# Other accumulators in a Strassen-like down projection, with the halves of the contraction exchanged

## The chip, the cores and the metric

One core of a Trainium2 chip runs the whole program. The metric is the device time of one execution in microseconds, as the median of several runs. Five engines matter: TensorE (PE, with its weight loads as PEld), VectorE (DVE), ScalarE (ACT), GpSimd (POOL) and SyncE (SP), which issues most of the DMAs. Each works through its own queue in a fixed order and waits for the others by semaphores.

## The reference, cut to what matters

An encoder of two layers runs on 512 + 256 tokens with 1024 channels. Each layer has two feed-forward blocks around a token mixer, so there are four in all:

```python
def swiglu_ffn(x, w1, w2):
    gate, up = jnp.split(x @ w1, 2, axis=-1)
    return (jax.nn.silu(gate) * up) @ w2

x = x + 0.5 * swiglu_ffn(rmsnorm(x, norm_g[li, 0]), ffn_w1[li, 0], ffn_w2[li, 0])
...
x = x + 0.5 * swiglu_ffn(rmsnorm(x, norm_g[li, 2]), ffn_w1[li, 1], ffn_w2[li, 1])
```

Here `w1` is 1024 x 5632 and `w2` is 2816 x 1024, in fp32. The change is in the second product, hidden @ w2, and in how its operands are laid out.

## The kernel before

**Precision.** Each fp32 operand is split into a high and a low part: ACT casts the high part (L199 for weights, L266 for activations) and DVE subtracts it from the value for the low part (L200, L267). A product of two operands is three matmuls: high by high, high by low, low by high.

**Seven products for eight.** The 768 tokens are halved (H = 384, that is HB = 3 blocks of 128), and so are the contraction and the outputs. A product of 2 x 2 blocks is made of seven block products, p1 to p7, as in Strassen's method in Winograd's form. Some operands are plain blocks, others are sums of blocks. On the activation side `FACTOR` (L45) names them: p1, p2 and p3 take the plain blocks b00, b10 and b11; p5, p6, p7 and p4 take t1, t2, t3 and t4, which `mix` (L348) makes with four subtractions, each followed by a split. In `b{j}{half}`, j is the half of the contraction and `half` the half of the tokens. Block b01 is used only inside the sums.

On the weight side `quad_steps` (L172) gets four raw tiles, a11, a12, a21 and a22, and three sums are made by accumulating DMAs that POOL issues (`into`, L140): two tiles s3 += a11, and a21 += a22. Seven steps then split one weight each. Two of them alter a tile for later steps: `p1` splits a11 and then adds a21 to it (L206); `p2` splits a12 and then adds a11 to it (L210). So p3, which splits a12, has the right value only after p1 and p2; p4 splits a22, p5 the sum in a21, p6 the altered a11, p7 the two s3 tiles.

**Staging.** Weights are staged in the order in which they were planned. `ahead` (L244), called by `done` whenever a product has used its weight, stages the next one as long as no more than WBUFS = 8 tiles are held. A weight of the up projection takes one tile, one of the down projection two. Raw tiles are four (RAWBUFS), and a down quad needs all four; they come free as the steps that read them are done, and then SP loads the next quad (L151).

**Up projection.** `up_pair` (L431) makes gate and up for one block of 128 hidden channels: seven products of 12 matmuls (L421) into four PSUM banks, with copies, sums, the Silu (L442, L454) and the multiplications (L449, L455) between. It yields two tiles, the first token half before its last product, the second after it. Four such tiles (two channel blocks, two token halves) go through `put` and `mix` as one part `kp` of the operands of the down projection.

**Down projection.** Every 512 hidden channels make a group (five in each feed-forward, 20 in all), and `down_quad` (L458) multiplies them by their rows of w2: seven products in the order `DOWN`, each of 3 token blocks x 2 parts x 3 = 18 matmuls (L479). After each product and block, `add_x` (L501, DVE) adds the bank, times 0.5 or -0.5, into a quarter of x. Three products continue in the bank of an earlier one, so that the sum of both is added to another quarter: p2 continues p1, p4 continues p5, and p3 continues p7. A continuing product must wait until `add_x` has read the bank. x is held in a transformed state over the five groups of a feed-forward: in the first group DVE alters two quarters (L464, L465), in the last it takes this back (L494, L495).

The order in which the engines get their instructions is fixed when the program is built. It follows the code, but an instruction that the builder reckons ready may be set ahead of one that waits.

Of the kernel before, what the change touches and what calls it, by code (L numbers as in the profile page):

```python
# [35 lines left out]
HB = H // P  # L36
# [4 lines left out]
SLOTS = 21  # L41
RING = 1024
UP = ("p1", "p7", "p2", "p5", "p4", "p6", "p3")
DOWN = ("p1", "p2", "p5", "p4", "p7", "p6", "p3")
FACTOR = {"p1": "b00", "p2": "b10", "p3": "b11", "p4": "t4", "p5": "t1", "p6": "t2", "p7": "t3"}  # L45


class Trunk:
# [291 lines left out]
    def put(self, name, kp, src):  # L340
        t = self.ops[(name, kp)] = self.big([P, 2, 2, H], F32R)
        self.split(src, t[:, :, 0, :], t[:, :, 1, :])
# [5 lines left out]
    def mix(self, b11, b12, b21, b22, put):  # L348
        sub = self.nc.vector.tensor_sub
        sub(b22, b12, b22)  # L350
        sub(b12, b11, b12)
        put("t1", b12)
        sub(b11, b11, b22)
        sub(b21, b21, b11)  # L354
        put("t4", b21)
        put("t3", b22)
        put("t2", b11)

    def sums(self):
        for kp in range(2):  # L360
# [17 lines left out]
    def plan_ffn(self, tag, w1, w2):  # L378
        def up(i):
            gate, up = (w1[:, c * P : (c + 1) * P] for c in (i, NF + i))  # L380
            if i < PLAIN:
                self.plan((tag, i, 0), gate, (NC, P))
                self.plan((tag, i, 1), up, (NC, P))
            else:
                self.plan_quad((tag, i), (gate, up), (NC, P), UP)

        for g in range(GROUPS):
            for i in range(4 * g, 4 * g + 4):
                up(i)
            rows = w2[4 * g * P : (4 * g + 4) * P, :].rearrange("(a k p) c -> k p a c", p=P, k=2)  # L390
            srcs = [rows[k][:, :, c * 512 : (c + 1) * 512] for c in range(2) for k in range(2)]
            self.plan_quad((tag, "down", g), srcs, (2, 512), DOWN)
        for i in range(NF - 2, NF):
            up(i)
        for c in range(2):
            self.plan((tag, "last", c), w2[(NF - 2) * P :, c * 512 : (c + 1) * 512], (2, 512))
# [61 lines left out]
    def down_quad(self, tag, g, hid):  # L458
        nc = self.nc
        cols = lambda b, c: self.x[b][:, c * 512 : (c + 1) * 512]  # L460
        if g == 0:
            for i in range(HB):
                x12, x21, x22 = cols(HB + i, 0), cols(i, 1), cols(HB + i, 1)
                nc.vector.tensor_add(x12, x12, x22)  # L464
                nc.vector.tensor_sub(x21, x21, x22)  # L465
        banks = {}
        for name in DOWN:
            wh, wl = self.take((tag, "down", g, name))
            chain = {"p2": "p1", "p4": "p5", "p3": "p7"}.get(name, name)
            for i in range(HB):  # L470
                if name == chain:
                    banks[(chain, i)] = self.ps()
                ps = banks[(chain, i)]
                sl = slice(i * P, (i + 1) * P)
                for kp in range(2):
                    h = hid[FACTOR[name]]
                    a, w = (h[:, kp, 0, sl], h[:, kp, 1, sl]), (wh[:, kp, :], wl[:, kp, :])
                    for q, (x, y) in enumerate(((0, 0), (0, 1), (1, 0))):
                        nc.tensor.matmul(  # L479
                            ps,  # L480
                            a[x],
                            w[y],
                            start=name == chain and kp == 0 and q == 0,
                            stop=kp == 1 and q == 2,
                            skip_group_check=True,
                        )
                x22 = cols(HB + i, 1)
                dst = {"p2": cols(i, 0), "p4": cols(i, 1), "p3": cols(HB + i, 0)}.get(name, x22)
                self.add_x(dst, ps, -0.5 if name in ("p1", "p5") else 0.5)
            self.done((tag, "down", g, name))  # L490
        if g == GROUPS - 1:
            for i in range(HB):
                x12, x21, x22 = cols(HB + i, 0), cols(i, 1), cols(HB + i, 1)
                nc.vector.tensor_sub(x12, x12, x22)  # L494
                nc.vector.tensor_add(x21, x21, x22)  # L495

    def add_x(self, x, ps, c):
# [5 lines left out]
    def ffn(self, tag, next_row):  # L503
        for g in range(GROUPS):
            hid = {}

            def put(name, src, kp):
                if name not in hid:
                    hid[name] = self.big([P, 2, 2, H], F32R)
                self.split(src, hid[name][:, kp, 0, :], hid[name][:, kp, 1, :])  # L510

            def gather(ts, kp):
                self.mix(ts[0], ts[1], ts[2], ts[3], lambda name, src: put(name, src, kp))

            if g == 0:
                ts = {}
                for half in range(2):
                    for j in range(PLAIN):
                        t = ts[2 * j + half] = self.up_plain(tag, j, half)
                        name = f"b{j}{half}"  # L520
                        if name != "b01":
                            put(name, t, 0)
                gather(ts, 0)
                self.run_later(len(self.deferred))
            for kp in range(2):
                if g == 0 and kp == 0:
                    continue
                ts = []
                for j in range(2):
                    for half, t in enumerate(self.up_pair(tag, 4 * g + 2 * kp + j)):  # L530
                        ts.append(t)
                        name = f"b{j}{half}"
                        if name != "b01":
                            put(name, t, kp)
                gather(ts, kp)
            self.down_quad(tag, g, hid)
        hids = []
        for j in range(NF - 2, NF):
            hid = self.big([P, 2, T], F32R)
            for half, t in enumerate(self.up_pair(tag, j)):  # L540
                self.split(t, *(hid[:, i, half * H : (half + 1) * H] for i in range(2)))
            hids.append(hid)
        if next_row is None:
            self.load_final()
        banks = {}

        def add(b, k, hid):
            sl = slice(b * P, (b + 1) * P)
            for c in range(2):
                wh, wl = self.take((tag, "last", c))  # L550
                if k == 0:
                    banks[(b, c)] = self.ps()
                w = wh[:, k, :], wl[:, k, :]
                self.mm3(banks[(b, c)], (hid[:, 0, sl], hid[:, 1, sl]), w, k == 0, k == 1)
                if b == NBLK - 1 and k:
                    self.done((tag, "last", c))

        for b in range(NBLK):
            for i, k in (((0, 0), (1, 0), (0, 1)), ((1, 1),))[b] if b < 2 else ((b, 0), (b, 1)):
                add(i, k, hids[k])  # L560
            for c in range(2):
                self.add_x(self.x[b][:, c * 512 : (c + 1) * 512], banks[(b, c)], 0.5)
            self.after_block(b, next_row)
            if b >= 4:
                self.run_later()
# [716 lines left out]
```

## Time and profile before

| What | Value |
|---|---|
| median of 3 runs | 2859.53 us (2858.35 to 2859.78) |
| the profiled execution | 2859.59 us |
| its span, first to last instruction | 2857.8 us |
| TensorE clock granted, mean | 0.997 |
| ACT busy | 1317.9 us (46%) |
| casts of weight halves on ACT (L199, w<-wr) | 415.9 us, 600 of 707 ns |
| low halves of weights on DVE (L200, w<-wr) | 438.9 us, 520 of 854 ns |
| up projection's matmuls (L421) | 6720 |

A group of instructions in the profile is named by line, engine and operation, with what it writes and reads (`x<-ps,x` reads a PSUM bank and x and writes x). Behind the bar stand its busy time, the mean length of one, and the idle time of its engine just ahead of such instructions, with what ended most of it. In a timeline each row has its start and length in us, and in brackets the idle time before it. The length of a matmul is from start to modelled end; successive matmuls overlap, so what a product takes is read from starts, not from lengths. "issue" as a releaser means that the trace shows nothing else that the engine waited for.

### The profile page before, as it was taken

The page shows a single profiled execution, that of the slowest core. Times are in us where ns is not written, and L with a number is a line of the kernel's source. Part 1 is how long each engine was busy: PE and PEld are TensorE (multiplying, and loading weights), DVE is VectorE, ACT ScalarE, POOL GpSimd, SP SyncE. Part 2 cuts the span into 40 slices and gives each one's busy share as a digit, 9 for nine tenths or more (in the row PEclk, how much of TensorE's full clock was granted, in tenths as well). Part 3 has the DMA queues.
Part 4 walks back from the last instruction along what each step waited for, and adds up shares of the span by engine and source line. Part 5 has one row for each costly group of instructions (what it writes and reads, how often), then busy time and mean ns, then how long its engine had stood idle before and what let it go on. Part 6 is the DMA issues. An engine that isn't in the chain of part 4 may idle for free. (4 is left out here: it accounts for less than half of the span.)

```text
span 2857.8 us, 40567 instructions
## 1 busy us (share of the span) xinstructions
PE 2804.0 (98%) x15225; PEld 2556.4 (89%) x15225; DVE 2175.1 (76%) x3750; ACT 1317.9 (46%) x2454; POOL 358.4 (13%) x402
## 2 busy tenths in 40 slices
PE   8999999999999999999999999999999999999998
PEld 8889999889899889998998998999887779989997
DVE  7788787477577658878878877887847868778877
ACT  7344443434344435434444543444457755434443
POOL 1111111000000001111111111111002211111110
PEclk9999999999999999999999999999999999999999
DMA  6554454311111133554444355444412113554443
GB/s 164 127 124 122 117 136 120 111 45 38 45 41 35 61 94 89 133 129 122 122 115 111 89 134 130 121 122 119 125 67 75 37 46 91 135 129 122 118 122 96
DMA packets 330102, 291.37 MB, mean 102 GB/s; under 512 B 11609, under 2 KB 257841, under 8 KB 329905
## 3 DMA queue, kind: packets, MB, share of 16 engines
q1 hardware_dynamic: 294064, 212.43, 25.2%
q0 software_dynamic: 31680, 62.93, 12.6%
q10 hardware_dynamic: 4160, 13.42, 1.3%
q8 instruction: 119, 1.95, 0.3%
q14 instruction: 79, 0.64, 0.1%
HBM read 216.39 MB, written 9.44 MB: 79 GB/s over the span
## 5 line engine op out<-in xcount | busy, mean ns | idle before, releaser
L421 PE MATMUL ps<-big,w 128*128 128x384 f32 x6720 | 1173.1, 334 | 3.1 <-DVE tA L444 3.0
L421 PEld LDWEIGHTS ps<-big,w 128*128 128x128 f32 x6720 | 1165.4, 188 | 9.0 <-DVE tA L444 7.3
L199 ACT CAST w<-wr 128x512 fp32r<-128x512 f32 x600 | 415.9, 707 | 722.6 <-PE ps L421 320.6
L479 PE MATMUL ps<-w,big 128*128 128x512 f32 x2520 | 586.5, 391 | 17.9 <-DVE x L501 17.8
L479 PEld LDWEIGHTS ps<-w,big 128*128 128x128 f32 x2520 | 469.6, 188 | 129.8 <-DVE x L501 17.4
L200 DVE TENSOR_TENSOR w<-wr,w 128x512 fp32r<-128x512 f32 (+1 forms) x520 | 438.9, 854 | 94.7 <-ACT w L199 86.1
L501 DVE SCALAR_TENSOR_TENSOR x<-ps,x 128x512 f32<-128x512 f32 x468 | 305.8, 683 | 20.8 <-PE ps L479 10.4
L141 POOL DMA_DIRECT2D s<-wr x120 | 105.6, 880 | 1333.9 <-DMA wr<-in_ffn_w_dram 590.5
L261 PE MATMUL ps<-w,big 128*128 128x512 f32 x624 | 249.9, 401 | 0.2
L263 PE MATMUL ps<-w,big 128*128 128x512 f32 x624 | 245.3, 393 | 1.3 <-DVE big L330 1.3
L262 PE MATMUL ps<-w,big 128*128 128x512 f32 x624 | 244.8, 392 | 0.0
L266 ACT CAST big<-tA 128x384 fp32r<-128x384 f32 x296 | 147.9, 512 | 175.6 <-DVE tA L449 72.4
L261 PE MATMUL ps<-big,w 128*128 128x384 f32 (+2 forms) x640 | 221.6, 347 | 2.1 <-ACT big L266 2.0
L262 PE MATMUL ps<-big,w 128*128 128x384 f32 (+2 forms) x640 | 217.4, 340 | 0.6 <-DVE big L267 0.5
L263 PE MATMUL ps<-big,w 128*128 128x384 f32 (+2 forms) x640 | 216.3, 338 | 0.0
L167 DVE TENSOR_TENSOR w<-wr,w 128x1024 fp32r<-128x1024 f32 x92 | 111.8, 1223 | 81.7 <-ACT w L166 57.7
L141 POOL DMA_DIRECT2D wr<-wr x100 | 87.2, 872 | 682.5 <-DVE tA L350 317.9
L267 DVE TENSOR_TENSOR big<-tA,big 128x384 fp32r<-128x384 f32 x296 | 164.2, 566 | 8.0 <-ACT big L266 4.6
L206 DVE TENSOR_TENSOR wr<-wr,wr 128x512 f32<-128x512 f32 (+1 forms) x100 | 79.4, 794 | 114.8 <-DMA wr<-wr 85.0
L166 ACT CAST w<-wr 128x1024 fp32r<-128x1024 f32 x92 | 96.6, 1052 | 122.2 <-PE ps L262 101.1
L263 PEld LDWEIGHTS ps<-w,big 128*128 128x128 f32 x624 | 117.7, 189 | 27.0 <-DVE big L330 2.0
L200 POOL TENSOR_TENSOR w<-wr,w 128x512 fp32r<-128x512 f32 x80 | 118.6, 1482 | 158.4 <-ACT w L199 145.3
(170 smaller groups left out, 3327.5 us busy)
## 6 DMA issues: line engine op xcount, KB each, us to landing
wr<-in_ffn_w_dram SPq DMA_DIRECT2D x264, 512.0 KB, 3.9
s<-in_ffn_w_dram SPq DMA_DIRECT2D x120, 256.0 KB, 3.0
s<-wr POOLq DMA_DIRECT2D x120, 256.0 KB, 3.8
wr<-wr POOLq DMA_DIRECT2D x80, 256.0 KB, 3.9
wr<-in_hg_w_in_dram SPq DMA_DIRECT2D x40, 512.0 KB, 3.8
wr<-wr POOLq DMA_DIRECT2D x20, 512.0 KB, 4.6
spill<-x ACTq DMA_DIRECT2D x12, 512.0 KB, 3.1
x<-spill ACTq DMA_DIRECT2D x12, 512.0 KB, 3.3
```

The costliest lines, as they stand in the source:

```text
L141: self.nc.gpsimd.dma_start(out, src, accum_op=ALU.add)
L167: self.nc.vector.tensor_sub(lo, raw, hi.bitcast(F32))
L199: nc.scalar.copy(h, src)
L200: (eng or nc.vector).tensor_sub(l, src, h.bitcast(F32))
L261: nc.tensor.matmul(out, a[0], b[0], start=first, stop=False)
L262: nc.tensor.matmul(out, a[0], b[1], start=False, stop=False)
L263: nc.tensor.matmul(out, a[1], b[0], start=False, stop=last)
L266: self.nc.scalar.copy(hi, src)
L267: self.nc.vector.tensor_sub(lo, src, hi.bitcast(F32))
L421: self.nc.tensor.matmul(ps, a[x], b[y], start=first and k == 0 and i == 0, stop=k == 3 and i == 2, skip_group_check=True,)
L479: nc.tensor.matmul(ps, a[x], w[y], start=name == chain and kp == 0 and q == 0, stop=kp == 1 and q == 2, skip_group_check=True,)
L501: self.nc.vector.scalar_tensor_tensor(x, ps, c, x, ALU.mult, ALU.add)
```

## The change

The halves of the contraction change roles: what was j = 0 is now j = 1, on both sides of the product. On the activation side `gather` hands the tiles to `mix` in exchanged order and `put` names the blocks `b{1 - j}{half}`; on the weight side the rows of w2 are read in exchanged order. With that, b10 and b11 (p2, p3) are made of the first channel block of a pair and b00 (p1) of the second block's first token half; the second block's second token half, the last to be ready, is the one that is used only in sums.

The products have another order and other chains: p3, p1, p2, p7, p5, p6, p4, where p7 now continues p3 (before, p3 continued p7). p1 is added with 0.5 where it was -0.5, p6 with -0.5, and the quarters of x in which the sums gather change with them. The order of staging is `DOWN_STAGED`, which differs from the order of use in that p3 comes after p1 and p2, since its weight is made by their steps. Before, both orders were the same. In `mix` each sum is put as soon as it is made, t3 first.

```diff
-DOWN = ("p1", "p2", "p5", "p4", "p7", "p6", "p3")
+DOWN = ("p3", "p1", "p2", "p7", "p5", "p6", "p4")
+DOWN_STAGED = ("p1", "p2", "p3", "p7", "p5", "p6", "p4")
...
         sub(b22, b12, b22)
         sub(b12, b11, b12)
+        put("t3", b22)
         put("t1", b12)
         sub(b11, b11, b22)
+        put("t2", b11)
         sub(b21, b21, b11)
         put("t4", b21)
-        put("t3", b22)
-        put("t2", b11)
...
-            srcs = [rows[k][:, :, c * 512 : (c + 1) * 512] for c in range(2) for k in range(2)]
-            self.plan_quad((tag, "down", g), srcs, (2, 512), DOWN)
+            srcs = [rows[1 - k][:, :, c * 512 : (c + 1) * 512] for c in range(2) for k in range(2)]
+            self.plan_quad((tag, "down", g), srcs, (2, 512), DOWN_STAGED)
...
-                nc.vector.tensor_add(x12, x12, x22)
                 nc.vector.tensor_sub(x21, x21, x22)
+                nc.vector.tensor_add(x22, x22, x12)
...
-            chain = {"p2": "p1", "p4": "p5", "p3": "p7"}.get(name, name)
+            chain = {"p2": "p1", "p4": "p5", "p7": "p3"}.get(name, name)
...
-                x22 = cols(HB + i, 1)
-                dst = {"p2": cols(i, 0), "p4": cols(i, 1), "p3": cols(HB + i, 0)}.get(name, x22)
-                self.add_x(dst, ps, -0.5 if name in ("p1", "p5") else 0.5)
+                dst = {"p2": cols(i, 0), "p4": cols(i, 1), "p7": cols(HB + i, 1)}.get(name, cols(HB + i, 0))
+                self.add_x(dst, ps, -0.5 if name == "p6" else 0.5)
...
-                nc.vector.tensor_sub(x12, x12, x22)
+                nc.vector.tensor_sub(x22, x22, x12)
                 nc.vector.tensor_add(x21, x21, x22)
...
-                self.mix(ts[0], ts[1], ts[2], ts[3], lambda name, src: put(name, src, kp))
+                self.mix(ts[2], ts[3], ts[0], ts[1], lambda name, src: put(name, src, kp))
...
-                        name = f"b{j}{half}"
+                        name = f"b{1 - j}{half}"
                         if name != "b01":
                             put(name, t, kp)
```

More of the change, by code (lines that the diff above doesn't have):

```diff
@@ L531, in ffn @@
                         ts.append(t)
-                        name = f"b{j}{half}"
+                        name = f"b{1 - j}{half}"
                         if name != "b01":
```

## The prediction

> **What bounds the kernel now.** I read the page's busy times first, then its groups, the waits of PE, and last the timeline of one down projection (group 1 of the first feed-forward, 174.43 to 204.74 us; the other 19 look alike).
>
> ```profile
> span 2857.8 us, 40567 instructions
> PE 2804.0 (98%) x15225; PEld 2556.4 (89%) x15225; DVE 2175.1 (76%) x3750; ACT 1317.9 (46%) x2454; POOL 358.4 (13%) x402
> L479 PE MATMUL ps<-w,big 128*128 128x512 f32 x2520 | 586.5, 391 | 17.9 <-DVE x L501 17.8
> L501 DVE SCALAR_TENSOR_TENSOR x<-ps,x 128x512 f32<-128x512 f32 x468 | 305.8, 683 | 20.8 <-PE ps L479 10.4
> ```
>
> PE is the bound. The down projection's 2520 matmuls (20 groups of 126) have 17.9 us of idle before them, and practically all of it ends with an add into x on VectorE (L501). No wait for a hidden sum (L266, L267) appears in that row: the operands that the reordering brings to the back hold PE up nowhere now.
>
> ```profile
> 174.43 4.28 PE L479 MATMUL ps<-w,big 128*128 128x512 f32 x18
> 179.24 10.24 PE L479 MATMUL ps<-w,big 128*128 128x512 f32 x44 [0.53 <-DVE x L501]
> 189.94 14.80 PE L479 MATMUL ps<-w,big 128*128 128x512 f32 x64 [0.47 <-DVE x L501]
> ```
>
> Columns: start, length, engine, line. A product is 18 matmuls (3 token blocks of 6). The last of a row runs 0.39 us, so the pitch is (14.80 - 0.39)/63 = 0.229 us and a product takes 4.12. The first break stands behind 18: p2 adds into p1's bank, which L501 must have read. The second stands behind 62 = 54 + 8: three products, then 8 matmuls of a later one (p7) that the built order pulled ahead of p4, which waits in the same way for the add of p5. By starts the breaks cost 179.24 - 174.43 - 18 x 0.229 = 0.69 and 189.94 - 179.24 - 44 x 0.229 = 0.62, 1.31 us a group: some 26 us in 20 groups, more than the 17.8 of the row, since PE also restarts slowly. That is all there is to win here.
>
> **Where the weights come from.** The same group, just ahead of its start:
>
> ```profile
> 164.54 0.88 POOL L141 DMA_DIRECT2D wr<-wr  x1 [10.19 <-DMA wr<-in_ffn_w_dram]
> 169.34 1.22 DVE L206 TENSOR_TENSOR wr<-wr,wr 128x1024 f32<-128x1024 f32 x1 [6.07 <-issue]
> 170.48 1.22 DVE L200 TENSOR_TENSOR w<-wr,w 128x1024 fp32r<-128x1024 f32 x1
> 171.62 0.55 DVE L444 TENSOR_TENSOR tA<-tA,ps 128x384 f32<-128x384 f32 x1
> 172.08 1.22 DVE L210 TENSOR_TENSOR wr<-wr,wr 128x1024 f32<-128x1024 f32 x1
> 173.22 1.22 DVE L200 TENSOR_TENSOR w<-wr,w 128x1024 fp32r<-128x1024 f32 x1
> 174.35 0.55 DVE L447 TENSOR_TENSOR tA<-tA,ps 128x384 f32<-128x384 f32 x1
> ...
> 164.08 1.05 ACT L199 CAST w<-wr 128x1024 fp32r<-128x1024 f32 x1
> 169.32 1.06 ACT L199 CAST w<-wr 128x1024 fp32r<-128x1024 f32 x1 [3.12 <-DMA wr<-wr]
> 172.02 1.05 ACT L199 CAST w<-wr 128x1024 fp32r<-128x1024 f32 x1 [1.64 <-PE ps L421]
> ```
>
> VectorE stands 6.07 us before L206 (a11 += a21), until the accumulating DMA a21 += a22, issued at 164.54, has landed; ACT's third cast waits for the same. Then come the low half of p2, L210 (a12 += a11), and the low half of the third weight (p5, cast at 169.32). So p1, p2, p5 are staged just before PE needs them, and p1, the first used, long before.
>
> **The change, part by part.**
>
> *p3 comes first but is staged third: +1.1 us a group.* p3's weight is a12 after L210, so its cast on ACT cannot begin before 172.08 + 1.22 = 173.30, where p5's began at 169.32. With some 0.05 for each hand-over: cast 173.35 to 174.40, low half 174.45 to 175.67 (1.22), usable at 175.72. PE is due at 174.43. Its first matmul (high by high) can go, the second needs the low half and is due at 174.66: 1.06, with the restart 1.1 us. Nothing else can fill it: p1's operand is now made of the hidden block whose product L449 comes later than this, and p2 follows p1 in its bank. Bounds: 0.6, if the built order issues the high matmuls of all three blocks first (two more, 0.46), and 2.3, if VectorE takes two or three of its 0.47 us steps (L447, L448, L451) ahead of the low half. I take 1.1 for 18 groups and 0.35 for two in which L206 starts 0.75 us earlier against PE:
>
> ```profile
> L206 DVE TENSOR_TENSOR wr<-wr,wr 128x512 f32<-128x512 f32 (+1 forms) x100 | 79.4, 794 | 114.8 <-DMA wr<-wr 85.0
> ...
> 80.34 1.23 DVE L206 TENSOR_TENSOR wr<-wr,wr 128x1024 f32<-128x1024 f32 x1 [5.71 <-DMA wr<-wr]
> 85.42 4.28 PE L479 MATMUL ps<-w,big 128*128 128x512 f32 x18
> ...
> 1629.10 1.23 DVE L206 TENSOR_TENSOR wr<-wr,wr 128x1024 f32<-128x1024 f32 x1 [4.83 <-DMA wr<-wr]
> 1634.93 5.24 PE L479 MATMUL ps<-w,big 128*128 128x512 f32 x22
> ...
> 2768.98 1.23 DVE L206 TENSOR_TENSOR wr<-wr,wr 128x1024 f32<-128x1024 f32 x1 [5.49 <-DMA wr<-wr]
> 2774.15 4.28 PE L479 MATMUL ps<-w,big 128*128 128x512 f32 x18
> ```
>
> (5.83 ahead at 1634.93, but 5.08 in the first of the 20 groups and 5.17 in the last; the wait of 114.8 us in all is 5.7 a group.) Sum 18 x 1.1 + 2 x 0.35 = 20.5 us.
>
> *p4 stands two products behind p5: -12.4 us.* p6's 4.12 us now lie between p5's last block and p4's first, and an add takes 0.68: the second break goes, 20 x 0.62. Likewise p7 comes two products behind p3, whose bank it continues; no new wait there.
>
> *p2 still follows p1 directly: +12 us.* It needs L501 on p1's first block. What VectorE does meanwhile:
>
> ```profile
> 177.94 0.55 DVE L453 TENSOR_TENSOR tA<-tA,ps 128x384 f32<-128x384 f32 x1
> 178.41 0.68 DVE L501 SCALAR_TENSOR_TENSOR x<-ps,x 128x512 f32<-128x512 f32 x1
> 179.08 0.56 DVE L455 TENSOR_TENSOR tA<-tA,tA 128x384 f32<-128x384 f32 x1
> ...
> 181.30 0.55 DVE L350 TENSOR_TENSOR tA<-tA,tA 128x384 f32<-128x384 f32 x1
> ...
> 185.80 0.56 DVE L267 TENSOR_TENSOR big<-tA,big 128x384 fp32r<-128x384 f32 x1
> 186.28 1.88 DVE L501 SCALAR_TENSOR_TENSOR x<-ps,x 128x512 f32<-128x512 f32 x3
> ```
>
> The adds of the first product slip in at 178.41 and after; then the sums of `mix` run from L350 to the last L267, and the adds of the second product wait until 186.28, though its first block was complete near 180.6. Before, that hurt nobody. Now the second product is p1, done near 174.43 + 1.1 + 36 x 0.229 = 183.8, and p2 waits for its add. In the same place, 1.2 us later because VectorE idles for p3's cast, 0.47 earlier because one put (a cast and an L267) moves from the tail into the pair before, it starts at 187.0 and ends at 187.7: 3.9 us behind p2's due time. p7 can stand in, as it did for p4 before: its operand is the first sum put, its bank was read long ago. With 8 of its matmuls pulled ahead (1.83 us) 2.1 are left, with all 18 none; those are the ends. The nearest row, the break behind 62, left 0.62 behind such a cover; with VectorE 1.2 - 0.47 = 0.73 later that is 1.35. I take 1.3 in place of 0.69: 20 x 0.61 = 12.2 us.
>
> *The rest: 0.* Matmuls, casts, adds and DMAs are as many as before (7 adds per block, 6 steps in the first and 6 in the last group of a feed-forward). The put that moves goes where VectorE waits 6 us for L206. p7 is now staged fourth, not fifth; its two raw tiles got their sums long before:
>
> ```profile
> 152.18 0.86 POOL L141 DMA_DIRECT2D s<-wr  x1 [6.56 <-DVE wr L210]
> ```
>
> Queued behind the late p3 low half on VectorE are L447 to L453 and the hidden sums; p1's operand, put after L449, is ready near 178.6, against p1 at 179.7.
>
> **Sum.** 20.5 - 12.4 + 12.2 = +20.3 us on the profiled execution's 2859.59 (span 2857.8 and 1.8 around it; the median of the three is 2859.53): 2880 us, +0.7%.
>
> **Rivals.**
>
> *Faster: the breaks go and nothing takes their place.* In the Trainium skill, "Perfetto Trace Analysis", section Matmuls, independent matmul groups should rotate through different PSUM banks, so that the evacuation of one lies beside the matmuls of the next. Two of the three chains (p3 to p7, p5 to p4) now have other products between their links, which is the mechanism of this rival; the trace agrees in so far as both breaks stand where two links of a chain touch (0.69 and 0.62 us). It wins 0.62 for p4 and, if p7 fills in before p2, 0.69 more. It decides the sign if p3's low half is done by 174.66, that is if L206 comes 1.1 us earlier against PE. For it: VectorE sits idle before L206, so all hangs on one DMA, and the row at 1629.10 shows 0.75 of those 1.1. Against it: in 18 of 20 groups L206 stands 5.1 to 5.5 ahead (the first and the last are quoted above), and the change touches nothing in front of that DMA. Time: 2859.6 - 26 = 2834, or 2846 if p2's break stays. Chance 0.13.
>
> *No change: p3 waits, the breaks go.* p7 covers p2 wholly: 20.5 - 26 = -5.5, 2854; with p3's wait at 1.3 or a rest of 0.3 at p2, up to 2864. For it: p7's operand comes first out of `mix` now. This is also the case that the change doesn't do what it says: no wait for sums was there to be taken away. Chance 0.19.
>
> *Slower still: the next weights come late.* a21 is freed by the low half of p5, which moves from third to fifth place, so one raw buffer of the next up quad is loaded later.
>
> ```profile
> 174.46 3.49 SPq L151 DMA_DIRECT2D wr<-in_ffn_w_dram  x2
> ...
> 182.44 0.89 POOL L141 DMA_DIRECT2D wr<-wr  x1 [17.02 <-DVE w L200]
> ...
> 196.17 0.69 DVE L206 TENSOR_TENSOR wr<-wr,wr 128x512 f32<-128x512 f32 x1
> wr<-wr POOLq DMA_DIRECT2D x80, 256.0 KB, 3.9
> ```
>
> Both loads issue by 177.95 now. p5 is staged once p3 is used up (179.7); its low half is done near 186, perhaps 187, 9 us later than the second load now. The accumulating DMA goes from 182.44 to 191.4, lands 0.9 + 3.9 later, at 196.2: just when L206 needs it. If it misses, VectorE stands with the adds of p5 and p6 behind it, and PE with p4: 1 to 2 us a group, 2900 to 2920. SP's queue holds that load ahead of others. Chance 0.10.
>
> **How the numbers follow.** Forecast (p3 late, p2 late, p4 free): 0.58, its own range 2866 to 2898 from the ends 0.6 to 2.3 and 0 to 2.1, which won't all fall on one side; 2880 predicted. Leaving out the lower part of the faster rival and the upper part of the last gives 2846 to 2900. About 0.2% (5.7 us) is what a measurement of this kernel tells from no change: faster is the first rival and a third of the second, 0.18; within, the rest of the second and the forecast's lower edge, 0.15; slower 0.67.
>
> **What would show it.** Of L479: a wait or slow start behind its first matmul in each group, ended by L200 on VectorE (p3's low half), about 1.1 us; one break near the 37th matmul or 8 later, ended by L501; none before p4. L206 should stand 5.1 us ahead of the group as now. If L479 idles for L200 nowhere, the first step is wrong and the time falls to 2834 to 2860; if L206 at the next up quad shows a wait for wr<-wr, it is the last rival.

## The result, and the profile after

The changed kernel takes 2878.65 us (median of 6 runs, 2876.18 to 2880.47) against 2858.94 for the kernel before in the same comparison: a ratio of 1.0071, with a 95% interval of 1.0059 to 1.0082. It is 0.7% slower; 2880 was predicted.

The lines of the page that answer to those shown of before. The change adds a line to the file, so L479 is now L480, L206 is L207, L210 is L211, L200 is L201, L444 is L445; L501 stays.

```profile
span 2878.7 us, 40608 instructions
PE 2801.8 (97%) x15225; PEld 2555.5 (89%) x15225; DVE 2185.1 (76%) x3750; ACT 1317.7 (46%) x2454; POOL 360.2 (13%) x402
L480 PE MATMUL ps<-w,big 128*128 128x512 f32 x2520 | 587.9, 392 | 40.9 <-DVE x L501 29.1
L501 DVE SCALAR_TENSOR_TENSOR x<-ps,x 128x512 f32<-128x512 f32 x468 | 306.5, 682 | 24.6 <-PE ps L480 13.3
```

PE's work is the same; the idle time before the down projection's matmuls went from 17.9 to 40.9 us. The waits of PE say what ended it (who waited for what, us in all, times, longest):

```profile
PE ps L480 <- DVE x L501: 29.1, 20, 1.5
PE ps L480 <- DVE w L201: 11.5, 19, 0.8
```

20 breaks end with an add into x, one in each group and longer than the 37 before; 19 new ones end with the low half of a weight. The timeline of group 1, first PE, then VectorE and ACT, shows where:

```profile
174.65 2.38 PE L422 MATMUL ps<-big,w 128*128 128x384 f32 x12 [0.74 <-DVE tA L445]
176.94 0.50 PE L480 MATMUL ps<-w,big 128*128 128x512 f32 x1
178.20 10.50 PE L480 MATMUL ps<-w,big 128*128 128x512 f32 x45 [0.76 <-DVE w L201]
190.16 18.47 PE L480 MATMUL ps<-w,big 128*128 128x512 f32 x80 [1.45 <-DVE x L501]
...
171.77 1.23 DVE L207 TENSOR_TENSOR wr<-wr,wr 128x1024 f32<-128x1024 f32 x1 [6.14 <-issue]
174.51 1.22 DVE L211 TENSOR_TENSOR wr<-wr,wr 128x1024 f32<-128x1024 f32 x1
175.84 1.05 ACT L200 CAST w<-wr 128x1024 fp32r<-128x1024 f32 x1 [7.66 <-DVE wr L211]
176.92 1.23 DVE L201 TENSOR_TENSOR w<-wr,w 128x1024 fp32r<-128x1024 f32 x1 [1.20 <-ACT w L200]
189.42 1.88 DVE L501 SCALAR_TENSOR_TENSOR x<-ps,x 128x512 f32<-128x512 f32 x3
```

One matmul, then a break until p3's low half is there (176.92 + 1.23 = 178.15; PE goes on at 178.20). Then 45 more: the rest of p3, all of p1 and, since 18 + 18 = 36 of these 46 belong to them, 10 of p7 pulled ahead. Then the break until the first add of p1 (189.42 + 0.68 = 190.10; PE goes on at 190.16). No third break: in front of p4 nothing waits any more.

By the starts of the matmuls, over all 20 groups (a break is what a start is late against the pitch of 0.228 us, restart included):

| us in 20 groups | before | after |
|---|---|---|
| behind p3's first matmul | - | 18.3 |
| in front of p2 | 13.2 | 34.5 |
| in front of p4 | 14.4 | 0 |
| length of the groups, sum | 596.6 | 620.8 |
| everything else up to the end of the last group | 2207.4 | 2204.1 |

The last row is the end of the last group, 2804.0 and 2824.9, less the sum above it. The groups lost 24.2 us, the rest won 3.3, together the 20.9 by which the span grew. The three breaks alone add up to 25.2 us more; the 1.0 us between that and the 24.2 lies spread over the starts of the 20 groups (0.05 us in each) and was not traced to anything.

### The profile page after: what moved, and what is told of

It reads as the page before. It is cut to its first block, busy times and chain, and to the rows that moved or that the text cites. A ratio compares the mean times of both kernels' runs of the same rounds, so it can differ in the third digit from the quotient of the medians.

```text
span 2878.7 us, 40608 instructions
## 1 busy us (share of the span) xinstructions
PE 2801.8 (97%) x15225; PEld 2555.5 (89%) x15225; DVE 2185.1 (76%) x3750; ACT 1317.7 (46%) x2454; POOL 360.2 (13%) x402
## 3 DMA queue, kind: packets, MB, share of 16 engines
q0 software_dynamic: 31680, 62.93, 12.5%
## 5 line engine op out<-in xcount | busy, mean ns | idle before, releaser
L422 PE MATMUL ps<-big,w 128*128 128x384 f32 x6720 | 1170.5, 334 | 2.1 <-DVE tA L445 2.1
L422 PEld LDWEIGHTS ps<-big,w 128*128 128x128 f32 x6720 | 1165.7, 188 | 5.1 <-DVE tA L445 3.2
L200 ACT CAST w<-wr 128x512 fp32r<-128x512 f32 x600 | 416.3, 706 | 793.6 <-PE ps L422 304.4
L480 PE MATMUL ps<-w,big 128*128 128x512 f32 x2520 | 587.9, 392 | 40.9 <-DVE x L501 29.1
L480 PEld LDWEIGHTS ps<-w,big 128*128 128x128 f32 x2520 | 469.9, 188 | 154.5 <-DVE x L501 37.5
L201 DVE TENSOR_TENSOR w<-wr,w 128x512 fp32r<-128x512 f32 (+1 forms) x520 | 417.5, 812 | 115.7 <-ACT w L200 106.5
L501 DVE SCALAR_TENSOR_TENSOR x<-ps,x 128x512 f32<-128x512 f32 x468 | 306.5, 682 | 24.6 <-PE ps L480 13.3
L207 DVE TENSOR_TENSOR wr<-wr,wr 128x512 f32<-128x512 f32 (+1 forms) x100 | 80.4, 804 | 100.7 <-DMA wr<-wr 74.5
L201 POOL TENSOR_TENSOR w<-wr,w 128x512 fp32r<-128x512 f32 x80 | 124.6, 1557 | 158.9 <-ACT w L200 145.3
```

What stands on the lines that cost most here:

```text
L200: nc.scalar.copy(h, src)
L201: (eng or nc.vector).tensor_sub(l, src, h.bitcast(F32))
L422: self.nc.tensor.matmul(ps, a[x], b[y], start=first and k == 0 and i == 0, stop=k == 3 and i == 2, skip_group_check=True,)
L480: nc.tensor.matmul(ps, a[x], w[y], start=name == chain and kp == 0 and q == 0, stop=kp == 1 and q == 2, skip_group_check=True,)
L501: self.nc.vector.scalar_tensor_tensor(x, ps, c, x, ALU.mult, ALU.add)
```

## The experiments

**1. p3 without its wait.** p3 takes its weight from a22, which no step alters, and p4 from a12, in the down projection only: the two swap their values. The work stays the same, but the sums are no longer those of the reference.

```diff
-            "p3": lambda: split("p3", [a12]),
-            "p4": lambda: split("p4", [a22]),
+            "p3": lambda: split("p3", [a12 if up else a22]),
+            "p4": lambda: split("p4", [a22 if up else a12]),
```

> The changed kernel, but in the down projection p3's weight is split from a22, which no step alters, and p4's from a12: the two swap their values, the work stays. Theory (p3 waits for L210, and VectorE's idling for that cast makes p2's break longer): the break behind the first matmul (0.9 us a group, 17.8 in all) goes, and VectorE is 1.2 us earlier, so that p2's break falls from 1.72 to about 0.6 us: 2878.7 - 17.8 - 22 = 2839 us. Rival 1 (p2's break comes from the place of p1's adds behind the hidden sums, not from VectorE's lateness): it stays 1.7, 2861 us. Rival 2 (p3's weight is late for want of tiles or a cast, not for L210): 2879 us.

Measured: 2853.51 us, 0.9984 of before (0.9974 to 0.9993). PE and L207 of group 1 and of group 0 in the timeline:

```profile
168.70 1.23 DVE L207 TENSOR_TENSOR wr<-wr,wr 128x1024 f32<-128x1024 f32 x1 [4.31 <-issue]
174.58 10.63 PE L480 MATMUL ps<-w,big 128*128 128x512 f32 x46
185.81 18.44 PE L480 MATMUL ps<-w,big 128*128 128x512 f32 x80 [0.60 <-DVE x L501]
...
80.92 1.22 DVE L207 TENSOR_TENSOR wr<-wr,wr 128x1024 f32<-128x1024 f32 x1 [6.63 <-DMA wr<-wr]
86.02 10.62 PE L480 MATMUL ps<-w,big 128*128 128x512 f32 x46
98.03 18.45 PE L480 MATMUL ps<-w,big 128*128 128x512 f32 x80 [1.40 <-DVE x L501]
```

The break behind the first matmul is gone in all 20 groups. So it came from the chain that ends with L210: in the timeline of the changed kernel above, ACT's cast of this weight is released by that addition (there L211). The break in front of p2 shrank from 34.5 to 25.6 us, less than the theory gave (about 12), more than the rival (34). What it depends on can be read from the two groups: where L207 starts 5.88 us ahead of the group the break is 0.60 by the row, where it starts 5.10 ahead it is 1.40. Lead and break add up to 6.48 and 6.50. By starts (the late start alone, without the slow restart behind it) their sum lies between 6.6 and 6.7 in all 20 groups: every 0.1 us by which L207 stands later against the group becomes 0.1 us of PE. The theory forgot that PE too had come 1 us later in the changed kernel, so that little of VectorE's 1.2 us showed.

**2. Distance for p4 alone.** The kernel before, with p7 used between p5 and p4 and nothing else changed; roles, chains and staging stay.

```diff
 DOWN = ("p1", "p2", "p5", "p4", "p7", "p6", "p3")
+DOWN_USED = ("p1", "p2", "p5", "p7", "p4", "p6", "p3")
...
-        for name in DOWN:
+        for name in DOWN_USED:
```

> The kernel before, with one edit: p7 is used between p5 and p4, the staging as it was. Theory (the break in front of p4 is only the add of p5 that p4 follows too closely): that break goes, 0.72 us in 20 groups, 2858.9 - 14.3 = 2845 us. Rival (VectorE is late all through the group, and the wait moves to the next product that needs an add): 2856 to 2859 us.

Measured: 2846.33 us, 0.9958 (0.9944 to 0.9973). The row of the page shows one break left, the one in front of p2:

```profile
L480 PE MATMUL ps<-w,big 128*128 128x512 f32 x2520 | 580.8, 390 | 8.9 <-DVE x L502 8.7
```

So distance between p5 and p4, which the change also brings, is worth 11.3 us by the medians (2857.64 for the kernel before in this comparison) and 14.4 by the breaks. Within the group the wait does not move on; outside it, the idle time before the up projection's matmuls went from 3.1 to 5.8 us.

**3. More distance for p2.** The changed kernel with the whole of p7 ahead of p2.

```diff
-DOWN = ("p3", "p1", "p2", "p7", "p5", "p6", "p4")
+DOWN = ("p3", "p1", "p7", "p2", "p5", "p6", "p4")
```

> The changed kernel with the whole of p7 between p1 and p2. Theory (p2's break is only the distance to p1's add, 4.1 us more of it are enough): the break of 1.72 us goes, 2878.7 - 34 = 2844 us, and the break behind the first matmul stays at 0.9. Rival (p7's own operand, or the bank of p5's third block, is late by as much as VectorE is): 2865 to 2879 us.

Measured: 2845.88 us, 0.9957 (0.9943 to 0.9972). Now only p3's break stands in the row:

```profile
L480 PE MATMUL ps<-w,big 128*128 128x512 f32 x2520 | 582.0, 391 | 10.1 <-DVE w L201 9.9
```

One word moved takes 33 us off the changed kernel and puts it ahead of the kernel before. The 10 matmuls of p7 that the built order had pulled ahead were too few; 18 are enough.

**4. Both breaks of the kernel before filled.** As experiment 2, and the first part (kp = 0) of p5, whose operand is ready since the pair before, between p1 and p2.

```diff
+DOWN_PARTS = (("p1", (0, 1)), ("p5", (0,)), ("p2", (0, 1)), ("p5", (1,)),
+    ("p7", (0, 1)), ("p4", (0, 1)), ("p6", (0, 1)), ("p3", (0, 1)))
...
-        for name in DOWN:
+        for name, kps in DOWN_PARTS:
...
-                for kp in range(2):
+                for kp in kps:
```

> The kernel before, with p7 between p5 and p4 and the first part (kp = 0) of p5 between p1 and p2; its operand is ready since the channel pair before. Theory (both breaks are only distance): both go, 2858.9 - 14.3 - 13.1 = 2831 us. Rival (VectorE's lateness moves on to a later product): 2845 us or more.

Measured: 2830.86 us, 0.9907 (0.9892 to 0.9922). PE in group 1:

```profile
172.14 28.76 PE L489 MATMUL ps<-w,big 128*128 128x512 f32 x126
200.75 4.52 PE L431 MATMUL ps<-big,w 128*128 128x384 f32 x25
```

126 matmuls in one row: the down projection runs without a break. From the first start of this group to that of the next row it takes 28.61 us, where it took 30.15.

**5. The additions made later in the code.** The kernel before, with L206 and L210 moved from the steps of p1 and p2 into those of p6 and p3.

```diff
         def p1():
             split("p1", [a11])
-            nc.vector.tensor_add(a11, a11, a21)
+            if up:
+                nc.vector.tensor_add(a11, a11, a21)
...
+        def p6():
+            if not up:
+                nc.vector.tensor_add(a11, a11, a21)
+            split("p6", [a11])
```

> The kernel before, but in the down projection the two additions to raw tiles (L206, L210) are made in the steps that need them, ahead of the splits of p6 and p3, not in those of p1 and p2; order of use as before. Theory (VectorE's 6 us wait for the accumulating DMA in front of L206 makes all its adds late, and both breaks come from that): both breaks go, 2857.6 - 13.1 - 14.3 = 2830 us. Rival 1 (only the first break hangs on it; the second is the distance from p5 to p4 behind a full VectorE): 2845 us. Rival 2 (VectorE is simply full in this stretch): 2855 to 2859 us. Rival 3 (a21 is held until p6's split, sixth instead of third, so the next raw tiles come late): above 2860 us.

Measured: 2857.74 us, 0.9999 (0.9989 to 1.0008), breaks as before. It tells nothing of the theory: the built order of VectorE's queue came out the same, row for row. The builder had set the two additions where they had been. The timeline shows it (L216 and L221 are the additions here):

```profile
167.59 1.22 DVE L216 TENSOR_TENSOR wr<-wr,wr 128x1024 f32<-128x1024 f32 x1 [5.98 <-issue]
170.34 1.22 DVE L221 TENSOR_TENSOR wr<-wr,wr 128x1024 f32<-128x1024 f32 x1
172.69 4.28 PE L491 MATMUL ps<-w,big 128*128 128x512 f32 x18
```

5.10 us ahead of the group, as in the kernel before. The same edit on top of experiment 4 changed nothing either.

> The kernel with both breaks filled by the order of use (part of p5 between p1 and p2, p7 between p5 and p4) and with the two additions made late as well. In the down projection nothing is left to win (28.37 us for 126 matmuls in every group); theory: only the waits of the up projection for L444 behind the late L206, 3.4 us in all, can go, 2827 to 2831 us. Rival (a21 held longer delays the next raw tiles): 2835 us or more.

Measured: 2830.69 us, 0.9900 (0.9886 to 0.9915), as experiment 4.

**6. The additions held back.** The same edit, and the first addition tied behind the last multiplication of the hidden block, so that VectorE cannot have it earlier. The order of use is that of the kernel before.

```diff
         def p6():
             if not up:
-                nc.vector.tensor_add(a11, a11, a21)
+                with self.tc.issue_after(self.last_dve):
+                    nc.vector.tensor_add(a11, a11, a21)
             split("p6", [a11])
```

> The kernel with the two additions (L206, L210) in the steps of p6 and p3, now also tied behind the last multiplication of the hidden block (L455), so that in VectorE's queue they stand after the adds of p2; in the run before this one the built order of VectorE came out the same as in the kernel before. Theory (VectorE's lateness at the start of a group, from the wait for the accumulating DMA and the two additions behind it, is what makes the breaks): VectorE reaches L453 2.3 us earlier, the first break goes (13.1 us) and the second shrinks from 0.72 to 0.1 or less although one addition (1.1 us) now stands ahead of p5's adds: 2831 to 2836 us. Rival 1 (distance alone, VectorE's start doesn't matter): 2857 us. Rival 2 (only the first break goes): 2844 us.

Measured: 2827.3 us, 0.9895 (0.9880 to 0.9909). It is the lowest median of all, but its interval overlaps that of experiment 4. VectorE and PE in group 1 (L200 is a weight's low half, L457 answers to L444, L460 to L447, L217 is the addition):

```profile
163.29 1.23 DVE L200 TENSOR_TENSOR w<-wr,w 128x1024 fp32r<-128x1024 f32 x1 [2.48 <-ACT w L199]
165.31 0.55 DVE L457 TENSOR_TENSOR tA<-tA,ps 128x384 f32<-128x384 f32 x1 [0.80 <-PE ps L434]
168.26 1.23 DVE L200 TENSOR_TENSOR w<-wr,w 128x1024 fp32r<-128x1024 f32 x1 [2.40 <-ACT w L199]
169.47 0.56 DVE L460 TENSOR_TENSOR tA<-tA,ps 128x384 f32<-128x384 f32 x1
171.35 28.79 PE L492 MATMUL ps<-w,big 128*128 128x512 f32 x126
183.32 1.22 DVE L217 TENSOR_TENSOR wr<-wr,wr 128x1024 f32<-128x1024 f32 x1
```

L460 starts 1.88 us ahead of the group, where L447 started 0.08 ahead in the kernel before (174.35 against 174.43). With the old orders, the old roles and the old chains both breaks are gone; what is left is 2.8 us by starts, in six groups, nearly all of it behind 108 matmuls (experiment 9 comes back to it). Distance was one way to hide the cause; the cause is that VectorE enters the group late, with two additions in its queue that nobody needs yet and that cannot begin before the accumulating DMA has landed. It is not the idle time as such: VectorE still idles 2.48 + 0.80 + 2.40 = 5.7 us ahead of this group, where it idled 6.07. But the low half of p2 and L457 are now done within that time, where L200 and L444 stood behind the first addition, and the two additions (1.2 us each) come after the adds of p2. How much of the gain is due to the work that went ahead, and how much to the additions that went behind, was not separated.

**7. A part of p1 ahead of p3.** The changed kernel, used in the order p1 (kp = 0), p3, p1 (kp = 1), p7, p2, p5, p6, p4, by the same edit as in experiment 4.

> The changed kernel with the first part (kp = 0) of p1 ahead of p3, its second part behind p3, then p7, p2, p5, p6, p4. p1's weight is staged first and its first part's operand is long ready, so 9 matmuls (2.06 us) stand in front of p3. Theory (p3's break is only that its weight is 0.9 us late, p2's only distance): both go, 2878.7 - 17.8 - 34.4 = 2826 us. Rival (p3's lateness passes on to the next product that needs VectorE): 2840 to 2846 us.

Measured: 2849.74 us, 0.9966 (0.9953 to 0.9979): the rival's account, though above its range of 2840 to 2846. p3's break went, but VectorE had to work as late as before, and 54 matmuls on, where p2 needs an add, PE met it again:

```profile
L490 PE MATMUL ps<-w,big 128*128 128x512 f32 x2520 | 582.7, 391 | 14.0 <-DVE x L513 14.0
```

**8. The order of the puts alone.** The changed kernel with the puts of `mix` as before (t1, t4, t3, t2).

> The changed kernel with the puts in mix in their former order (t1, t4, t3, t2); roles, chains and order of use stay changed. PE's built order is the same. Theory (p2's break hangs on p1's adds behind all the sums, p7 is ready in time either way): 2876 to 2881 us. Rival (p7 fills in for p2 only because t3 is put first; with t3 put later PE waits for L267 as well): 2885 to 2910 us.

Measured: 2879.57 us, 1.0072 (1.0056 to 1.0089): this part of the change does nothing to the time.

**9. Held back, and filled.** Experiments 4 and 6 together.

> The kernel before with the additions held back behind L455 and with the order of use that puts part of p5 between p1 and p2 and p7 between p5 and p4. Held back alone gave 2827.3 us, with 3.2 us of breaks left in the down groups (570.7 against 20 x 28.37 = 567.4). Theory: those go too, 2823 to 2826 us. Rival (a11 and a12 are altered late, so p6 and p3 are staged late whatever the order): 2827 us or more.

Measured: 2849.25 us, 0.9967 (0.9955 to 0.9980). The two don't add up; they spoil each other by over 20 us. One break stands in each group again, behind 103 matmuls, and its cause is new (L217 is the first addition of the next up quad, L526 the add into x):

```profile
194.74 0.69 DVE L217 TENSOR_TENSOR wr<-wr,wr 128x512 f32<-128x512 f32 x1 [1.40 <-issue]
195.35 1.88 DVE L526 SCALAR_TENSOR_TENSOR x<-ps,x 128x512 f32<-128x512 f32 x3
196.09 5.51 PE L502 MATMUL ps<-w,big 128*128 128x512 f32 x23 [0.79 <-DVE x L526]
```

VectorE stands idle in front of an addition to the next raw tiles, and the add that PE needs waits behind it (195.35 + 0.68 = 196.03; PE goes on at 196.09). Over all groups VectorE idles 28.7 us in front of this addition, against 0.6 in the kernel before. The likely reason is that the raw tile a21 is held until p6's split, so that the next raw tiles and their accumulating DMA come late: the third rival of the prediction, in another kernel. The row itself says only "issue", and holding a21 by itself was not tried.

But this wait is not new: experiment 6 has it too, 27.8 us in all, in group 1 at the same place (194.26 - 171.35 = 22.9 us into the group, here 194.74 - 171.74 = 23.0). In its timeline the addition is L207 and the add into x L514:

```profile
194.26 0.69 DVE L207 TENSOR_TENSOR wr<-wr,wr 128x512 f32<-128x512 f32 x1 [1.31 <-issue]
194.87 1.88 DVE L514 SCALAR_TENSOR_TENSOR x<-ps,x 128x512 f32<-128x512 f32 x3
```

There the first add behind the wait ends 24.2 us into the group, and PE, by the place of the breaks that are left, needs it after 108 matmuls (108 x 0.228 = 24.6): just in time in 14 of 20 groups. With the order of experiment 4 PE needs an add from behind the wait after 103 (23.5 us), and is late in all 20. So the two changes clash by where the order puts the need, not by a DMA that came later still.

## Why the prediction was right, point by point

*All there is to win is two breaks, and neither is a wait for a sum.* Right for the down projection. Experiment 4 removes both and takes 27 us off (26 said), and no operand of p5, p6, p7 or p4 showed up in any row of L479's waits. Experiment 6 found a little more outside it: by starts its groups are 26.0 us shorter than before, and the rest up to the end of the last group 5.8. The Trainium skill's rule in "Perfetto Trace Analysis", section Matmuls, that PSUM banks should rotate, holds as far as experiments 2 and 3 go (14.4 us before p4, 34.5 before p2, gone by distance). Experiment 6 gets both breaks away with the links as close as before, so the rule names a cover here, not the cause.

*p3 first, staged third: +20.5 us.* Right in mechanism and nearly in size. The steps came as worked out: cast begun 0.11 us after L211 ended, low half right behind the cast, VectorE idle 1.20 us for it, the second matmul 1.03 late (1.06 said), with the restart 1.14. The sum is 18.3, since the break was shorter in nine groups, with a longer lead of L207 (up to 5.9 us), not in two. Experiment 1 shows that the wait is for the chain through L210.

*p4 two products behind p5: -12.4 us.* Right; 14.4 by starts, and experiment 2 has it alone.

*p2 behind p1: +12.2 us.* Right in mechanism, mis-sized: +21.3 (34.5 against 13.2). VectorE's part was right: p1's adds were to start 187.0 - 174.43 = 12.6 us into the group, behind the hidden sums, and started 189.42 - 176.94 = 12.5 into it. What was taken wrongly is how much of p7 would stand in. The ends were 2.1 us (8 matmuls) and 0 (18); the value of 1.3 was taken between them, by the break that 8 matmuls had left behind p5. 10 were pulled ahead, and 1.7 was left. The prediction's own sum had this value in reach: 3.9 us behind the due time, less 10 x 0.229, is 1.6, and the restart makes it 1.7. The step that was mis-sized is that it went by the other break instead.

*The rest: 0.* It was -3.3 us, outside the groups. The row of the up projection's weight loads has the size of it: idle time before them 9.0 us before and 5.1 after, of which 7.3 and 3.2 ended with the subtraction at L444 (now L445).

```profile
L421 PEld LDWEIGHTS ps<-big,w 128*128 128x128 f32 x6720 | 1165.4, 188 | 9.0 <-DVE tA L444 7.3
L422 PEld LDWEIGHTS ps<-big,w 128*128 128x128 f32 x6720 | 1165.7, 188 | 5.1 <-DVE tA L445 3.2
```

That of the matmuls themselves (L421, now L422) fell less, from 3.1 to 2.1 us, so the row does not prove it, and why L444 is less late wasn't tested. So +20.3 was forecast, and the terms measured by starts are 18.3 + 21.3 - 14.4 - 3.3 = +21.9, of which the span shows 20.9. That the total was hit so closely is luck in part: the errors, +9.1 for p2 and -7.5 for the other three, nearly cancelled.

*The rivals.* Faster: its condition, an L206 that comes 1.1 us earlier, was not met in any group (the longest lead was 5.9 us). Experiment 1, in which p3 no longer waits, did turn the sign (0.9984), but to 2853.5 and not to 2846 or 2834, since p2's break stayed at 25.6 us. No change by p7's cover: would have needed 18 of p7, as experiment 3 shows with 2846. Late weights: not in this kernel (VectorE idles 0.9 us in all before L207 at the next up quads, 0.6 before the change); experiments 6 and 9 have that wait. Three small slips of the working change nothing: p4's break alone is worth 12.4 us, so the faster rival with p2's break left gives 2847; 2864 needs both of the two conditions named for it; and 0.13 + 0.19/3 is 0.19, not 0.18.

## What to carry to other kernels

Before reordering PE's work around a wait, look at why the engine that ends the wait is late: here two additions that were not yet needed stood in VectorE's queue behind a wait of 6 us for a DMA, with needed work behind them, and moving them (2827 us) did as much without any reordering as the best order of use did (2831). An operand that is used first should be staged first: of the chain of updates that makes it (a DMA, two additions, a cast, a subtraction) PE sees all that lies behind its own arrival, up to 1.0 us a group here. And look at the order that was built, not at the order of the code: the same addition moved in the code alone changed no queue.

## What the runs showed that was not expected

Two fixes of the same breaks, worth 27 and 30 us each, gave 9.5 together: the one makes VectorE wait some 23 us into the group, where PE hardly notices, and the other makes PE need an add from there some 1.1 us (5 matmuls) earlier. And where PE does wait for VectorE, nothing absorbs a delay: over 20 groups of experiment 1, VectorE's lead at the start and PE's break ten microseconds later add up to the same 6.6 to 6.7 us.
